# Modulation products of a two-layer diffusion trunk: fp32 in four 32-column quarters of the array, and sums of squares asked for three microseconds later

## Chip, cores and metric

The kernel runs on one core of one Trainium2 chip. The metric is the device time of one execution in microseconds (us): the median of three runs of the kernel before is 3194.48 us (3193.29 to 3196.1).

## What is computed

Two layers over 1024 latent tokens and 256 context tokens of width 1024, in fp32. Each layer modulates a normalised input with a shift, a scale and a gate that come from a condition vector: `c` for the latent tokens, `c_ctx` for the context. The parts that the change touches are the modulation and the sums of squares of the q/k normalisation:

```python
def rmsnorm(u, g):
    u32 = u.astype(jnp.float32)
    y = u32 * lax.rsqrt(jnp.mean(u32 * u32, axis=-1, keepdims=True) + EPS)
    return (y * g.astype(jnp.float32)).astype(u.dtype)

def modulation(cond, w_mod, b_mod):
    m = jax.nn.silu(cond) @ w_mod + b_mod
    shift, scale, gate = jnp.split(m, 3, axis=-1)
...
for l in range(DEPTH):
    sh_l, sc_l, gt_l = modulation(c, w_mod[l], b_mod[l])
    sh_c, sc_c, gt_c = modulation(c_ctx, w_mod[l], b_mod[l])
    h_lat = rmsnorm(x, norm_g[l]) * (1.0 + sc_l) + sh_l
    h_ctx = rmsnorm(ctx, norm_g[l]) * (1.0 + sc_c) + sh_c
    q_l, k_l, v_l, ga_l, u_l, gb_l, gm_l = split_proj(h_lat @ w_in[l])
...
    q_l = axial_rope(rmsnorm(q_l.reshape(B, n, N_Q_HEADS, HEAD_DIM), q_norm_g[l]), rows, cols) * scale
    k_l = axial_rope(rmsnorm(k_l.reshape(B, n, N_KV_HEADS, HEAD_DIM), k_norm_g[l]), rows, cols)
...
    x = x + gt_l * merge_branches(o_lat, ga_l, lru_l, gb_l, gm_l, w_a_out[l], w_b_out[l], w_out[l])
```

So a layer's modulation is a product of two condition vectors with a 1024 x 3072 weight matrix, six column blocks of 512: blocks 0 and 1 are the shift, 2 and 3 the scale, 4 and 5 the gate.

## The kernel before

Everything is laid out with features on the 128 partitions; the tokens are three chunks, L0 and L1 (512 latent tokens each) and C (256 context tokens). Large products split each fp32 operand into a high and a low fp32r part and sum three fp32r products, `gemm`, in groups of three matmuls per 128 rows of the contraction.

The stages follow each other. *Preparation* loads x and layer 0's modulation weights, normalises, modulates, and begins the q projections. Then for each layer *q/k/v*, *recurrent*, *attention* and *output* (in two halves: A for L0 and C, B for L1), with the next layer's preparation woven into the output stage.

What sets the order of the work: TensorE's order is the order in which the program emits it (`manual_schedule`). A `Timeline` counts modelled TensorE time in `tl.now`; `tl.at(delay, fn)` holds back a piece of work, and `tl.pump()` emits what is due. So a delay decides how many matmuls stand ahead of a piece on TensorE. All transfers are issued in order by one queue (SP). Buffers come from rings in turn: `mix` (four tiles) and `sm` (three); a new tile waits for the last use of the one whose place it takes.

Names and lines of the kernel before that the following speaks of:

- Preparation. `modulation` (line 318) multiplies the condition vectors `cs` (two columns of the array) with one 512-row half of a 512-column block per call, four fp32 products of 512 columns into the PSUM tile `modps`. `mod_turn` (line 332) copies the two result rows to `mrow`, and TensorE turns them by transposes into `modpt`; `mod_done` (line 307) adds the bias and makes the multipliers `ma`. Preparation does blocks 0, 2, 1, 3 from eight weight tiles `wm` of 1024 KB. `scale_rows` (line 627) makes L0's, C's and L1's sums of squares (`sqa`, `ssn`), the reciprocal roots (`rst`), their broadcast (`rb`) and scales x; `modulate` (line 662) makes the high and low operand `h` or `c`.
- Output stage. `modulation_side` (line 345) does 16 half-blocks of 256 columns: layer 0's gate (blocks 4, 5) and all six blocks of layer 1. For each, ScalarE multiplies eight weight tiles with the condition (`macc`, `wmt`, line 358), GpSimd adds them up (line 360), ScalarE and VectorE split the sum (`mhi`, `mlo`, lines 367 and 368), and TensorE sums over the partitions with four fp32r products of 256 columns. It is a generator: `weave` (line 598) takes one step of it per two groups of three matmuls in half A, and 0.36 steps per group in half B.
- q/k. `Group.evac` (line 461) copies a projection (`qg`) and squares it (`sqq`) on ScalarE; `sums` (line 476) sums the squares per head on TensorE (`ssq`) in the four 32-column quarters, 4.0 us of modelled time after the last chunk; then `qrow` goes through DRAM, `rsqrt_small` makes `rst` (line 400 is its square root on ScalarE), and `apply` (line 519) rotates and scales. `lsum` (line 1045) sums attention rows (`lps`), also in quarters.
- `recurrent_consts` (line 194) makes constants in `spt`, some 26 small VectorE instructions per layer.

Of the kernel before, what the change touches and what calls it, by code (L numbers as in the profile page):

```python
# [26 lines left out]
F32 = mybir.dt.float32  # L27
# [12 lines left out]
KT = 8  # L40
# [60 lines left out]
def trunk_kernel(ctx: ExitStack, tc: tile.TileContext, xT, cc, par, wmod, win, wgate, wo,  # L101
# [45 lines left out]
    def tr(o, a):  # L147
# [10 lines left out]
    e2 = sm("e2")  # L158
    V.memset(e2[:, 0:4], 0.0)
    V.memset(e2[:, 0:4:3], 1.0)  # L160
    cond_sel = const.tile([128, 2, 2], F32R, name="condsel")
    V.tensor_copy(cond_sel, e2[:, 0:4].rearrange("p (a b) -> p a b", a=2))
# [9 lines left out]
                    pattern=[[-1, 128]], channel_multiplier=1)  # L172

# [7 lines left out]
    cs = const.tile([128, KT, 2], F32, name="cs")  # L181
    ct = const.tile([128, KT, 2], F32, name="ct")
    S.activation(ct, cc_sb, AF.Tanh, scale=0.5)
    V.scalar_tensor_tensor(cs, ct, 1.0, cc_sb, op0=OP.add, op1=OP.mult)
    V.tensor_scalar(cs, cs, 0.5, None, op0=OP.mult)
# [8 lines left out]
    def recurrent_consts(l):  # L194
        lam = p(l, "lam", 0, 16)
        t = const.tile([128, 6, 16], F32, name="spt", tag="spt")
# [124 lines left out]
    def modulation(l, i, b, half, wm, box):  # L321

        if half == 0:
            box["ps"] = ptile("s", "modps")
        ps = box["ps"]
        for k in range(4):
            mm(ps[0:2], cs[:, 4 * half + k], wm[:, k], half == 0 and k == 0, half == 1 and k == 3)
            tl.pump()
        if half == 1:
            mod_turn(l, 4 * b, 4, ps, 1.0)  # L330

    def mod_turn(l, i, n, ps, wait):

        row = sm("mrow")
        S.activation(row[0:2, 0:n * 128], ps[0:2, 0:n * 128], AF.Copy)

        def turn():
            pt = ptile("s", "modpt")
            for j in range(n):
                tl.now += 0.109  # L340
                nc.tensor.transpose(pt[:, 2 * j:2 * j + 2], row[0:2, j * 128:(j + 1) * 128], ident[0:2, 0:2])
            mod_done(l, i, n, pt)

        tl.at(wait, turn)

    def modulation_side(l, blocks, work):

        for hb in [2 * b + i for b in blocks for i in range(2)]:
            acc = work.tile([128, 2, 256], F32, name="macc", tag="macc")
            for k in range(KT):  # L350
                if k % 4 == 0:
                    wm = mix("wm")[:, 0:1024].rearrange("p (k n) -> p k n", k=4)
                    DMA.dma_start(wm, wmod[l, k * 128:(k + 4) * 128, hb * 256:(hb + 1) * 256]
                                  .rearrange("(k p) n -> p k n", p=128))
                w = wm[:, k % 4]
                t = acc if k == 0 else sm("wmt").rearrange("p (s n) -> p s n", s=2)
                for s in range(2):
                    S.activation(t[:, s], w, AF.Copy, scale=cs[:, k, s:s + 1])  # L358
                if k:
                    G.tensor_add(acc, acc, t)  # L360
                yield

            for _ in range(4):
                yield
            hi = sm("mhi", F32R).rearrange("p (s n) -> p s n", s=2)
            lo = sm("mlo", F32R).rearrange("p (s n) -> p s n", s=2)
            S.activation(hi, acc, AF.Copy)
            V.tensor_sub(lo, acc, r32(hi))
            for _ in range(3):
                yield  # L370
            ps = ptile("av", "modps")
            for x, part in enumerate((hi, lo)):
                for s in range(2):
                    mm(ps[0:2, 0:256], cond_sel[:, s], part[:, s], x + s == 0, x + s == 2)
            mod_turn(l, 2 * hb, 2, ps, 3.0)
# [76 lines left out]
    class Group:  # L452
# [10 lines left out]
        def evac(self, i, c, ps):  # L463
            off, n = CH[c]
            if i not in self.qg:
                self.qg[i] = mix("qg")
            S.activation(self.qg[i][:, off:off + n], ps[:, :n], AF.Copy, scale=self.g)
            part = next(p_ for p_ in self.parts if c in p_)
            o = min(CH[x][0] for x in part)
            if (i, o) not in self.sq:  # L470
                self.sq[i, o] = self.work().tile([128, TOK], F32, name="sqq", tag="sqq") if self.work else mix("sqq")
            S.activation(self.sq[i, o][:, off - o:off - o + n], ps[:, :n], AF.Square)
            if c == part[-1]:
                tl.at(4.0, lambda: self.sums(i, part, o))
# [134 lines left out]
    with tc.tile_pool(name="prep", bufs=1, reuse_waits="tile") as work:  # L609
        xs, arrive = {}, {}  # L610
# [15 lines left out]
        def scale_rows(c):  # L626
# [18 lines left out]
            def bcast():  # L645
# [4 lines left out]
                for k in range(KT):  # L650
                    if c == "L1":
# [10 lines left out]
        def modulate(c, k0, nk=4):  # L662

            n = CH[c][1]
# [28 lines left out]
        for i in range(8):  # L693
            tl.now = max(tl.now, arrive[i])
            modulation(0, i, blocks[i // 2], i % 2, xs[i], box)
            if i == 4:
                tl.at(0.0, lambda: modulate("L0", 0))
            if i == 6:
                tl.at(0.0, lambda: modulate("C", 0))
# [9 lines left out]
    for l in range(DEPTH):  # L709
# [414 lines left out]
        with tc.tile_pool(name="outp", bufs=1, reuse_waits="tile") as work:  # L1124
# [128 lines left out]
            else:  # L1253
                mod_start(l + 1)
                side = modulation_side(l, (4, 5), work) if l == 0 else iter(())
                tl.fill(weave(ga, itertools.chain(side, modulation_side(l + 1, (0, 2, 1, 3), work)), 0.5))
            tl.fill(halves(1, nxt) if last else weave(halves(1, nxt), modulation_side(l + 1, (4, 5), work), 0.36))
# [79 lines left out]
```

## Time and profile before

| | |
|---|---|
| time, median of 3 runs | 3194.48 us |
| the profiled execution's own time | 3197.96 us |
| its span | 3196.2 us |
| TensorE (PE) busy | 3059.7 us, 96% |
| VectorE (DVE) busy | 2457.1 us, 77% |
| ScalarE (ACT) busy | 1749.6 us, 55% |
| GpSimd (POOL) busy | 1020.0 us, 32% |
| first projection on PE | at 51.00 us |
| output stage of layer 0, 1350 to 1610 us | PE busy 239.74 of 260.00 us |
| end of layer 1's q/k/v, 1760 to 1905 us | PE busy 134.75 of 145.00 us |

The profile is of one execution; times in it count from the start of its span. PE is busy nearly always, so what matters is where it is not, and where it runs at the lower of its two clock levels (1.2 instead of 2.4 GHz, shown as 0.50 of full speed). An engine's row names an instruction's output and inputs; an fp32 matmul appears as two records.

### The profile page before, as it was taken

What the parts mean: (1) busy time and instruction counts of PE and PEld (TensorE: products, weight loads), DVE (VectorE), ACT (ScalarE), POOL (GpSimd) and SP (SyncE); (2) the same over time, 40 slices, a digit from 0 to 9 for tenths busy, and PEclk for the clock granted to TensorE, in tenths of its full rate; (3) what the DMA queues carried; (4) which work ended last, traced back from release to release, by engine and by line L of the source; (5) the groups of instructions that cost most, each with busy time, mean ns of one, the idle gap of its engine ahead of it and who ended that gap; (6) DMA issues with size and microseconds to landing.
All of it is one profiled execution on the core that took longest, in us unless ns stands there. A gap on an engine that the chain in (4) does not pass through costs nothing. (4 is left out here: it accounts for less than half of the span.)

```text
span 3196.2 us, 42921 instructions
## 1 busy us (share of the span) xinstructions
PE 3059.7 (96%) x14880; PEld 2430.8 (76%) x14880; DVE 2457.1 (77%) x3675; ACT 1749.6 (55%) x3060; POOL 1020.0 (32%) x777
## 2 busy tenths in 40 slices
PE   7999999999999999999899999899999999999999
PEld 3788788777777777787778778777777777777887
DVE  7665887589898988556685785997799999996544
ACT  4323667466666666545555324676477766673222
POOL 0211444234434333234432121433244444441000
PEclk9999999999999999999999999999999999999999
DMA  5443111311222122264555452111412121115554
GB/s 196 144 152 121 50 50 62 115 59 59 73 64 78 60 64 64 87 195 153 172 191 168 147 166 87 60 47 53 121 56 75 58 75 58 52 59 170 181 177 138
DMA packets 233049, 331.95 MB, mean 104 GB/s; under 512 B 53296, under 2 KB 99184, under 8 KB 232576
## 3 DMA queue, kind: packets, MB, share of 16 engines
q1 hardware_dynamic: 232832, 329.21, 32.0%
q8 instruction: 117, 1.92, 0.2%
q14 instruction: 100, 0.82, 0.1%
HBM read 252.54 MB, written 76.58 MB: 103 GB/s over the span
## 5 line engine op out<-in xcount | busy, mean ns | idle before, releaser
L145 PE MATMUL gps<-h,whi 128*128 128x512 f32 x3328 | 1041.4, 394 | 21.1 <-DVE g L876 15.3
L145 PEld LDWEIGHTS gps<-h,whi 128*128 128x128 f32 x3328 | 612.1, 190 | 148.4 <-issue 10.7
L1004 DVE TENSOR_TENSOR pl<-pf,ph 128x512 fp32r<-128x512 f32 x656 | 630.2, 961 | 83.1 <-ACT ph L1003 79.5
L145 PE MATMUL gps<-h,wlo 128*128 128x512 f32 x1664 | 654.5, 393 | 1.3 <-DVE wlo L227 1.3
L1002 ACT ACTIVATE pf<-s2ps 128x512 f32<-128x512 f32 x656 | 392.8, 599 | 348.1 <-issue 157.0
L1018 POOL TENSOR_TENSOR acc<-pf 128x512 f32<-128x512 f32 x256 | 352.0, 1375 | 713.1 <-ACT pf L1002 711.5
L980 DVE TENSOR_REDUCE mp<-s1ps 128x1 f32<-128x512 f32 (+1 forms) x800 | 454.1, 583 | 63.7 <-PE s1ps L145 60.8
L1003 ACT ACTIVATE ph<-s2ps 128x512 fp32r<-128x512 f32 x656 | 390.0, 595 | 0.0
L227 DVE TENSOR_TENSOR wlo<-wraw,whi 128x512 fp32r<-128x512 f32 x392 | 335.3, 878 | 61.4 <-ACT whi L226 32.7
L226 ACT ACTIVATE whi<-wraw 128x512 fp32r<-128x512 f32 x324 | 193.6, 627 | 333.8 <-PE gps L145 258.1
L145 PEld LDWEIGHTS gps<-h,wlo 128*128 128x128 f32 x1664 | 314.3, 189 | 69.9 <-DVE wlo L227 2.0
L145 PE MATMUL s1ps<-k,qa 128*128 128x512 f32 (+1 forms) x800 | 284.9, 363 | 12.3 <-DMA qa<-q0L 10.3
L145 PE MATMUL avps<-ph,vv 128*128 128x512 f32 x656 | 266.9, 407 | 0.0
L145 PE MATMUL avps<-pl,vv 128*128 128x512 f32 x656 | 260.2, 397 | 5.0 <-DVE pl L1004 4.9
L145 PE MATMUL s2ps<-qa,k 128*128 128x512 f32 x656 | 261.1, 398 | 1.8 <-DVE mp L980 1.6
L145 PE MATMUL s2ps<-qb,k 65*128 65x512 f32 x656 | 260.3, 397 | 0.0
L145 PE MATMUL gps<-e,whi 128*128 128x512 f32 x768 | 243.9, 399 | 0.2 <-DVE e L227 0.2
L360 POOL TENSOR_TENSOR macc<-macc,wmt 128x512 f32<-128x512 f32 x112 | 156.2, 1395 | 255.2 <-ACT wmt L358 221.9
L145 PE MATMUL qps<-h,whi 128*128 128x512 f32 x640 | 203.0, 398 | 1.5 <-DVE h L674 0.9
L1020 POOL TENSOR_TENSOR acc<-acc,pf 128x512 f32<-128x512 f32 x128 | 181.5, 1418 | 71.4 <-ACT pf L1002 69.2
L145 PE MATMUL gps<-c,whi 128*128 128x256 f32 x1024 | 197.2, 288 | 3.1 <-DVE c L222 2.1
L145 PEld LDWEIGHTS s1ps<-k,qa 128*128 128x128 f32 x800 | 151.6, 190 | 51.8 <-issue 6.4
(216 smaller groups left out, 5026.6 us busy)
## 6 DMA issues: line engine op xcount, KB each, us to landing
wraw<-in_win_dram SPq DMA_DIRECT2D x200, 256.0 KB
wraw<-in_wo_dram SPq DMA_DIRECT2D x192, 256.0 KB
wm<-in_wmod_dram SPq DMA_DIRECT2D x32, 512.0 KB
wm<-in_wmod_dram SPq DMA_DIRECT2D x8, 1024.0 KB
rb<-rq SPq DMA_DIRECT2D x64, 128.0 KB
k<-k SPq DMA_DIRECT2D x24, 320.0 KB
v<-vst SPq DMA_DIRECT2D x20, 256.0 KB
vv<-v SPq DMA_DIRECT2D x8, 640.0 KB
```

The source lines that it names most:

```text
L145: nc.tensor.matmul(o, a, b, start=start, stop=stop)
L226: S.activation(dst_hi, src, AF.Copy)
L227: (V if lo_eng == "v" else G).tensor_sub(dst_lo, src, r32(dst_hi))
L360: G.tensor_add(acc, acc, t)
L980: tl.at(0.3, lambda: V.reduce_max(self.mp[:, j, b:b + 1], ps[:, :n], axis=AX.X))
L1002: S.activation(pf, ps, AF.Exp)
L1003: S.activation(ph, ps, AF.Exp)
L1004: tl.at(1.4, lambda: V.tensor_sub(pl, pf, r32(ph)))
L1018: G.tensor_add(self.acc_tile(x), first, pf)
L1020: G.tensor_add(self.accs[x], self.accs[x], pf)
```

## The change

- Both modulations become fp32 products with `csp`, the condition padded with zeros to 32 columns. Four products, one per 128 rows, go to the four 32-column quarters of the array and leave four partial results on PSUM partitions 0, 32, 64 and 96. `mrow` is now 128 rows, and the turn is an fp32 product of `mrow` with `sel4`, which adds the four parts.
- In the output stage ScalarE's scaling, GpSimd's additions and the high/low split go; each half-block is two weight tiles loaded a few steps earlier, eight products of 256 columns, and the turn. A half-block takes 14 steps of the generator instead of 15.
- `sums` is asked for 7.0 instead of 4.0 us after the last chunk.
- In preparation `modulate("L0", 0)` comes after call 5 instead of 4 and `modulate("C", 0)` after the last call.
- `cs`, `ct` and `spt` come from the `sm` ring, so the small VectorE instructions of `recurrent_consts` run in each layer's q/k stage instead of at the start of the kernel.

```diff
-    e2 = sm("e2")
-    V.memset(e2[:, 0:4], 0.0)
-    V.memset(e2[:, 0:4:3], 1.0)
-    cond_sel = const.tile([128, 2, 2], F32R, name="condsel")
-    V.tensor_copy(cond_sel, e2[:, 0:4].rearrange("p (a b) -> p a b", a=2))
...
+    sel4 = const.tile([128, 2], F32, name="sel4")
+    V.reduce_sum(sel4, ident.rearrange("p (g s) -> p s g", s=32)[:, 0:2], axis=AX.X)
...
-    cs = const.tile([128, KT, 2], F32, name="cs")
-    ct = const.tile([128, KT, 2], F32, name="ct")
+    cs, ct = (sm(n_)[:, 0:16].rearrange("p (k s) -> p k s", k=KT) for n_ in ("cs", "ct"))
     S.activation(ct, cc_sb, AF.Tanh, scale=0.5)
     V.scalar_tensor_tensor(cs, ct, 1.0, cc_sb, op0=OP.add, op1=OP.mult)
-    V.tensor_scalar(cs, cs, 0.5, None, op0=OP.mult)
+    csp = const.tile([128, KT, 32], F32, name="csp")
+    V.memset(csp, 0.0)
+    V.tensor_scalar(csp[:, :, 0:2], cs, 0.5, None, op0=OP.mult)
...
-        t = const.tile([128, 6, 16], F32, name="spt", tag="spt")
+        t = sm("spt")[:, 0:96].rearrange("p (a b) -> p a b", a=6)
...
-    def modulation(l, i, b, half, wm, box):
-
+    def mod_half(ps, half, wm, n):
+
+        for k in range(4):
+            mm(ps[32 * k:32 * k + 32, :n], csp[:, 4 * half + k], wm[:, k], half == 0, half == 1, 0.215 * n / 512)
+
+    def modulation(l, b, half, wm, box):
         if half == 0:
             box["ps"] = ptile("s", "modps")
-        ps = box["ps"]
-        for k in range(4):
-            mm(ps[0:2], cs[:, 4 * half + k], wm[:, k], half == 0 and k == 0, half == 1 and k == 3)
-            tl.pump()
+        mod_half(box["ps"], half, wm, 512)
+        tl.pump()
         if half == 1:
-            mod_turn(l, 4 * b, 4, ps, 1.0)
+            mod_turn(l, 4 * b, 4, box["ps"], 1.0)
     def mod_turn(l, i, n, ps, wait):
         row = sm("mrow")
-        S.activation(row[0:2, 0:n * 128], ps[0:2, 0:n * 128], AF.Copy)
+        S.activation(row[:, 0:n * 128], ps[:, 0:n * 128], AF.Copy)
         def turn():
             pt = ptile("s", "modpt")
             for j in range(n):
-                tl.now += 0.109
-                nc.tensor.transpose(pt[:, 2 * j:2 * j + 2], row[0:2, j * 128:(j + 1) * 128], ident[0:2, 0:2])
+                mm(pt[:, 2 * j:2 * j + 2], row[:, j * 128:(j + 1) * 128], sel4, True, True, 0.2)
             mod_done(l, i, n, pt)
         tl.at(wait, turn)
-    def modulation_side(l, blocks, work):
+    def modulation_side(l, blocks):
         for hb in [2 * b + i for b in blocks for i in range(2)]:
-            acc = work.tile([128, 2, 256], F32, name="macc", tag="macc")
-            for k in range(KT):
-                if k % 4 == 0:
-                    wm = mix("wm")[:, 0:1024].rearrange("p (k n) -> p k n", k=4)
-                    DMA.dma_start(wm, wmod[l, k * 128:(k + 4) * 128, hb * 256:(hb + 1) * 256]
-                                  .rearrange("(k p) n -> p k n", p=128))
-                w = wm[:, k % 4]
-                t = acc if k == 0 else sm("wmt").rearrange("p (s n) -> p s n", s=2)
-                for s in range(2):
-                    S.activation(t[:, s], w, AF.Copy, scale=cs[:, k, s:s + 1])
-                if k:
-                    G.tensor_add(acc, acc, t)
-                yield
-
+            wms = []
+            for half in range(2):
+                wm = mix("wm")[:, 0:1024].rearrange("p (k n) -> p k n", k=4)
+                DMA.dma_start(wm, wmod[l, half * 512:half * 512 + 512, hb * 256:(hb + 1) * 256]
+                              .rearrange("(k p) n -> p k n", p=128))
+                wms.append(wm)
+                for _ in range(3):
+                    yield
             for _ in range(4):
                 yield
-            hi = sm("mhi", F32R).rearrange("p (s n) -> p s n", s=2)
-            lo = sm("mlo", F32R).rearrange("p (s n) -> p s n", s=2)
-            S.activation(hi, acc, AF.Copy)
-            V.tensor_sub(lo, acc, r32(hi))
-            for _ in range(3):
+            ps = ptile("av", "modps")
+            for half in range(2):
+                mod_half(ps, half, wms[half], 256)
+            mod_turn(l, 2 * hb, 2, ps, 3.0)
+            for _ in range(4):
                 yield
-            ps = ptile("av", "modps")
-            for x, part in enumerate((hi, lo)):
-                for s in range(2):
-                    mm(ps[0:2, 0:256], cond_sel[:, s], part[:, s], x + s == 0, x + s == 2)
-            mod_turn(l, 2 * hb, 2, ps, 3.0)
...
-                tl.at(4.0, lambda: self.sums(i, part, o))
+                tl.at(7.0, lambda: self.sums(i, part, o))
...
-            modulation(0, i, blocks[i // 2], i % 2, xs[i], box)
-            if i == 4:
+            modulation(0, blocks[i // 2], i % 2, xs[i], box)
+            if i == 5:
                 tl.at(0.0, lambda: modulate("L0", 0))
-            if i == 6:
-                tl.at(0.0, lambda: modulate("C", 0))
+        tl.at(1.0, lambda: modulate("C", 0))
         tl.at(1.2, lambda: modulate("L0", 4))
         tl.at(4.0, lambda: modulate("C", 4))
...
-                side = modulation_side(l, (4, 5), work) if l == 0 else iter(())
-                tl.fill(weave(ga, itertools.chain(side, modulation_side(l + 1, (0, 2, 1, 3), work)), 0.5))
-            tl.fill(halves(1, nxt) if last else weave(halves(1, nxt), modulation_side(l + 1, (4, 5), work), 0.36))
+                side = modulation_side(l, (4, 5)) if l == 0 else iter(())
+                tl.fill(weave(ga, itertools.chain(side, modulation_side(l + 1, (0, 2, 1, 3))), 0.5))
+            tl.fill(halves(1, nxt) if last else weave(halves(1, nxt), modulation_side(l + 1, (4, 5)), 0.36))
```

The rows are in each engine's own order. TensorE in preparation (`modps` modulation products, `modpt` turns, `ssn` sums of squares, `rb` their broadcast, `qps` the first projection). Before:

```order
L145 MATMUL ssn<-ones,sqa 128x1 x4
L145 MATMUL modps<-wm,cs 2x512 x2
L145 MATMUL rb<-ident,rst 128x128 x4
L145 MATMUL modps<-wm,cs 2x512 x2
L341 MATMUL modpt<-ident,mrow 128x2 x4
L145 MATMUL modps<-wm,cs 2x512 x7
L341 MATMUL modpt<-ident,mrow 128x2 x4
L145 MATMUL ssn<-ones,sqa 128x1 x2
L145 MATMUL modps<-wm,cs 2x512 x2
L145 MATMUL rb<-ident,rst 128x128 x2
L145 MATMUL modps<-wm,cs 2x512 x5
L145 MATMUL qps<-h_530,whi 128x512
```

and now:

```order
L145 MATMUL ssn<-ones,sqa 128x1 x4
L145 MATMUL modpt<-sel_91,mrow 128x2 x4
L145 MATMUL rb<-ident,rst 128x128 x4
L145 MATMUL modps<-wm,csp 32x512 x8
L145 MATMUL modpt<-sel_91,mrow 128x2 x4
L145 MATMUL ssn<-ones,sqa 128x1 x2
L145 MATMUL modps<-wm,csp 32x512 x4
L145 MATMUL rb<-ident,rst 128x128 x2
L145 MATMUL qps<-h_539,whi 128x512
L145 MATMUL qps<-h_540,whi 128x512
L145 MATMUL qps<-h_539,wlo 128x512
L145 MATMUL modpt<-sel_91,mrow 128x2 x4
```

L0's `ssn` now has five of the eight weight tiles' products ahead of it (20 products, where 14 were), the turn of block 2 stands ahead of `rb`, and the last turn follows the first group of the projection.

TensorE in the output stage, around the first half-block (`gps` are the output products of C; the half-block's turn follows later). Before:

```order
L145 MATMUL gps<-c_13880,whi 128x256
L145 MATMUL gps<-c_13879,wlo 128x256
L145 MATMUL modps<-mhi,condsel 2x256 x2
L145 MATMUL modps<-mlo,condsel 2x256 x2
L145 MATMUL gps<-c_13879,whi 128x256
```

and now, one such place some 33 matmuls earlier:

```order
L145 MATMUL gps<-c_13879,whi 128x256
L145 MATMUL gps<-c_13878,wlo 128x256
L145 MATMUL modps<-wm,csp 32x256 x8
L145 MATMUL gps<-c_13878,whi 128x256
L145 MATMUL gps<-c_13879,whi 128x256
```

The products no longer read `mhi` and `mlo` but the loaded weight tile `wm`, and there are eight of them at a time.

ScalarE at the end of layer 1's q/k/v (`qg` and `sqq` copy and square the last k projection, `rst` is the square root of a norm that went through DRAM, `vst` copies v). Before:

```order
L467 ACTIVATE qg<-qps,par 128x512
L472 ACTIVATE sqq<-qps 128x512
L467 ACTIVATE qg<-qps,par 128x256
L472 ACTIVATE sqq<-qps 128x256
L400 ACTIVATE rst<-rst 128x20
L467 ACTIVATE qg<-qps,par 128x512
L472 ACTIVATE sqq<-qps 128x512
L764 ACTIVATE vst<-vps 128x4x64
```

and now:

```order
L388 ACTIVATE rst<-rst 128x16
L455 ACTIVATE qg<-qps,par 128x512
L460 ACTIVATE sqq<-qps 128x512
L471 ACTIVATE qrow<-ssq 128x320
L455 ACTIVATE qg<-qps,par 128x256
L460 ACTIVATE sqq<-qps 128x256
L455 ACTIVATE qg<-qps,par 128x512
L460 ACTIVATE sqq<-qps 128x512
L388 ACTIVATE rst<-rst 128x20
L753 ACTIVATE vst<-vps 128x4x64 x2
```

The last `qg` and `sqq` of 512 columns stood behind the second `rst` and now stand ahead of it.

## Rows read from the trace of the kernel before

**Rows 1.** Whom PE waited for, whole span (us in total, times, longest us).

```profile
PE ssq L145 <- ACT sqq L472: 16.8, 6, 7.8
PE modps L145 <- ACT mhi L367: 9.1, 6, 4.8
PE modps L145 <- DVE mlo L368: 5.6, 6, 2.6
```

**Rows 2.** Timeline of PE, output stage: first and last of those twelve waits.

```profile
1458.50 0.59 PE L145 MATMUL modps<-mhi,condsel 128*2 128x256 f32 x2 [4.80 <-ACT mhi L367]
1608.64 0.40 PE L145 MATMUL modps<-mlo,condsel 128*2 128x256 f32 x2 [0.41 <-DVE mlo L368]
```

**Rows 3.** Stretches after a PE wait: busy times, granted clock (PEclk), DMA.

```profile
1458.50:1463.30 4.80, 4.57 (x21) 3.98 (x22) 2.22 (x5) 3.40 (x8) 1.20 (x1) 0.50 0.18 61
1552.00:1559.00 7.00, 5.99 (x26) 5.71 (x27) 3.49 (x7) 2.41 (x6) 0.00 (x0) 0.51 0.47 164
1897.40:1903.40 6.00, 6.00 (x26) 4.97 (x27) 6.00 (x15) 1.03 (x3) 2.07 (x3) 0.50 0.28 104
```

**Rows 4.** Timeline of ScalarE and PE, end of layer 1's q/k/v (idle before).

```profile
1884.02 0.22 ACT L400 ACTIVATE rst<-rst 128x16 f32<-128x16 f32 x1 [12.71 <-issue]
...
1896.06 0.22 ACT L400 ACTIVATE rst<-rst 128x20 f32<-128x20 f32 x1 [9.80 <-issue]
...
1897.39 1.28 PE L145 MATMUL ssq<-sqq,sel 128*32 128x320 f32 x4 [7.80 <-ACT sqq L472]
```

**Rows 5.** Timeline, preparation and the start of the projections, in order of time.

```profile
22.29 1.28 ACT L400 ACT_TABLE_LOAD   x1
...
28.04 4.87 DVE L654 TENSOR_TENSOR xsL<-xsL,rb 128x512 f32<-128x512 f32 x8 [1.69 <-PE rb L145]
...
51.00 0.74 PE L145 MATMUL qps<-h,whi 128*128 128x512 f32 x2
...
80.31 0.53 PE L145 MATMUL ssq<-sqq,sel 128*32 128x192 f32 x8 [2.97 <-ACT sqq L472]
...
86.56 0.62 PE L145 MATMUL qps<-h,whi 128*128 128x512 f32 x2
```

**Rows 6.** VectorE in preparation (busy time, count, PE's clock, DMA).

```profile
28.00:83.00 55.00, 46.42 (x107) 0.89 0.31 111
```

**Rows 7.** Groups of PE, preparation (busy, mean ns, idle before and releaser).

```profile
L145 PE MATMUL modps<-wm,cs 128*2 128x512 f32 x64 | 33.5, 672 | 7.2 <-DVE spt L207 7.0 <-DMA wm<-in_wmod_dram 0.3
```

**Rows 8.** Timeline of PE: prices of fp32 products and what starts behind them.

```profile
24.05 1.05 PE L145 MATMUL ssn<-ones,sqa 128*128 128x1 f32 x8 [1.22 <-DVE sqa L395]
...
715.07 1.06 PE L145 MATMUL lps<-acc,ones 128*32 128x512 f32 x8
716.06 0.50 PE L145 MATMUL avps<-ph,vv 128*128 128x512 f32 x1
...
1402.65 0.39 PE L145 MATMUL modps<-mhi,condsel 128*2 128x256 f32 x2
...
1403.12 0.40 PE L145 MATMUL gps<-c,whi 128*128 128x256 f32 x2
...
1823.87 0.63 PE L145 MATMUL ssq<-sqq,sel 128*32 128x256 f32 x4 [0.58 <-ACT sqq L472]
1824.42 0.73 PE L145 MATMUL qps<-h,whi 128*128 128x512 f32 x2
```

**Rows 9.** Groups of PE, output stage: the turns of the 16 half-blocks.

```profile
L341 PE MATMUL modpt<-ident,mrow 2*128 2x2 f32 x32 | 4.5, 208 | 0.2 <-ACT mrow L335 0.2
```

**Rows 10.** Timeline, output stage: a weight tile's issue on SP and first use.

```profile
1350.29 0.38 SPq L353 DMA_DIRECT2D wm<-in_wmod_dram  x1
...
1354.25 0.91 ACT L358 ACTIVATE macc<-wm,cs 128x256 f32<-128x256 f32 x2 [2.53 <-DMA wm<-in_wmod_dram]
```

**Rows 11.** SP's own waits, 1350 to 1760 us (us in total, times, longest).

```profile
SPq L1171 <- ACT wmt L358: 30.4, 9, 6.0
```

**Rows 12.** The `spt` instructions alone, first 15 us (VectorE and ScalarE busy).

```profile
0.00:15.00 15.00, 8.78 (x52) 0.43 (x2) 1.00 0.88 309
```

More of the change, by code (lines that the diff above doesn't have):

```diff
@@ L609, in trunk_kernel @@
     with tc.tile_pool(name="prep", bufs=1, reuse_waits="tile") as work:
-        xs, arrive = {}, {}
+        xs, arrive, scaled = {}, {}, set()
         mod_start(0)
@@ L650, in bcast @@
                 for k in range(KT):
+                    scaled.add(c)
                     if c == "L1":
@@ L662, in modulate @@
         def modulate(c, k0, nk=4):
+            assert c in scaled
             n = CH[c][1]
```

## Prediction

> **What bounds the kernel now.** I read the waits of TensorE first, since it is busy 96% of the span: a gain is either a wait that goes, matmul time that shrinks, or time at the lower clock that is won back. Over the whole span three of its waits bear on this change [rows 1]. In the output stage the half-blocks' products wait for `mhi` 9.1 us in all and for `mlo` 5.6 us, twelve waits; the timeline shows the first of them at 1458.50 with 4.80 us, the last at 1608.64 [rows 2]. The reader should see who is late: the sum of scaled weights passes from ScalarE to GpSimd eight times and back, and TensorE, in order, stands with all output products queued behind it. In the q/k stages `ssq` waits for `sqq` 16.8 us in six waits, the longest 7.8 us.
>
> The stretches behind long waits come next [rows 3]: the granted clock is 0.50 of full speed, its 1.2 GHz level, after TensorE stood idle up to 1458.50, and again from 1552 and from 1897. So such a wait costs more than itself.
>
> Third, the 7.8 us wait [rows 4]. ScalarE is held at `rst` until 1884.02 (12.71 us) and again until 1896.06 (9.80 us), and the last square that `ssq` needs stands behind that second `rst`. TensorE starts again at 1897.39.
>
> Last, preparation [rows 5, 6, 7]. The 64 records of modulation products keep TensorE busy 33.5 us, and the projections begin at 51.00; but VectorE works 46.42 of the 55 us from 28 to 83, from the scaling of L0 to the last low part of L1, and the first tile's L1 product, which needs all of that, ends only at 86.56. I take VectorE to be the limit there.
>
> **The change, part by part.** All is summed against the profiled execution's 3197.96 us, which lies 3.48 us above the median of the three runs, and then moved down by that.
>
> *Output stage, what goes.* What the twelve waits were for goes: 9.1 + 5.6 = 14.7 us. The lost clock behind them: busy 4.57 us at 0.50 and 5.99 us at 0.51 [rows 3], so 4.57 x 0.50 + 5.99 x 0.49 = 5.2 us; a third such stretch is left out. ScalarE's scalings, GpSimd's additions and VectorE's `mlo` lie beside TensorE's other work and count for nothing more, though their relief may shorten other waits of this stage; I leave that to the range.
>
> *Output stage, what comes.* Eight fp32 products of 256 columns in quarters, per visit. Rows of that form exist [rows 8]: a set of four of 256 columns takes 1824.42 - 1823.87 = 0.55 us (`ssq`), a set of four of 512 takes 716.06 - 715.07 = 0.99 us (`lps`). So a column costs 1.72 ns per set and a set has 0.11 us beside. Two sets: 1.10 us. The old four products took 1403.12 - 1402.65 = 0.47 us: +0.63 us. The turn was 4.5 us for 16 visits [rows 9], 0.28 each; two fp32 products with a full stationary tile, at 1.05 / 4 = 0.26 each by `ssn` [rows 8], make 0.53: +0.25. Together +0.88 us x 16 = +14.1 us, all on TensorE's path. The stage's sum is -14.7 - 5.2 + 14.1 = **-5.8 us**; call it -6.
>
> Here a rule is to be weighed. The rows cannot tell whether the 0.11 us is paid for each set of four or once for each entry into quarters, since every set in the trace stands alone among full-array products. The Trainium skill, TensorEngine Tiling (Array Packing), Key Properties, says that changing the tiling mode drains the engine, while changing the tile does not. It speaks against the change, which enters and leaves that mode 16 more times in this stage; but it also says that two adjacent sets pay once. By it a visit would be 0.99 us and the sum -7.6 us instead of -5.8; no run here shows two sets in a row. I keep 1.10.
>
> The weight tiles must be there when the products come. A tile issued at 1350.29 was first used at 1354.25 after a wait for it [rows 10], so 4.0 us. The second tile is asked for 7 of 14 steps ahead; twelve visits took 1402.65 to 1608.64, about 18 us each, so roughly 8.7 us ahead at 14/15 of that pace. I cost this wait at nothing, with 4.7 us of cover; what happens without it is a rival.
>
> *Sums asked for later.* Of the 16.8 us, 2.97 are in preparation [rows 5] and counted there; 13.8 are left in five waits, and 6.00 us at 0.50 behind the longest lose 3.0 us. Three microseconds more of matmuls ahead of each `ssq` cover the four short waits (6.0 us together). For the long one: at the least 3 us go, the rest and the clock stay. At the most all 7.8 + 3.0 go, since in the changed order the last square stands ahead of the second `rst`, and has only to follow the first, released at 1884.02; the seven ScalarE instructions from there to the last square should be over before TensorE arrives, at 1897.39 - 7.80 + 3 = 1892.6. So 9.0 to 16.8 us; I take **-15**, near the upper end because of that order. The transfers behind `ssq` (`qrow` out and back on SP) move with it and the rotation on VectorE ends later; behind them stand the next tiles' weights, which are asked for two tiles ahead, and the recurrent stage, which needs no q or k. If that cover failed, it would come out as waits of the next tiles, up to the 3 us per shift.
>
> *Constants moved.* VectorE does 8.78 us of small `spt` instructions in the first 15 us [rows 12]; 4.4 us per layer now fall into q/k stages, and ScalarE must reload its function table twice per layer, 1.28 us each [rows 5]. Covered by VectorE's idle time there (the stage's VectorE is not what TensorE waits for) and by the 3 us that `ssq` gained. Zero; 7 us per layer at the worst, which the upper bound takes in part.
>
> *Preparation.* Eight calls fall from 33.5 us of TensorE to a set of four each, 0.99 us, or twice that at 1.2 GHz. But VectorE has the same instructions, 55 us from the scaling of L0 on. Its start cannot come sooner: `ssn` now stands behind one weight tile more and a turn stands ahead of `rb`, 0.99 + 1.05 us, doubled at the low level 4.1. The gain: some of VectorE's 8.6 us of idle time in that stretch ended on TensorE's products, and the 2.97 us wait of `ssq` may go; 3 us at the most. So -3 to +4; I take **+1**.
>
> Sum: -6 - 15 + 1 = -20. 3197.96 - 20 = 3178.0 profiled, **3174.5 us** as a median. About 0.2% (6.4 us) is what a measurement of this kernel can tell from no change.
>
> **Rivals.**
>
> *The late square stays late (0.17).* The first `rst` moves with its sums, later by 3 us or more, and holds ScalarE as long as before. For it: ScalarE was held twice in a row [rows 4], which is a slow chain through DRAM and not one accident. Against it: the order. The lower end, -9, applies: 3180.5 us.
>
> *Preparation was bound by TensorE (0.08).* For it: projections begin only at 51.00. Then the products' fall, and the 4 half-speed ones among them, brings the whole chain forward, -8 instead of +1: 3165.5 us. Against it: VectorE's 46 of 55 us.
>
> *Slower: the weight tiles come late (0.07).* They take places in the four-tile ring, each now held until TensorE has used it, where ScalarE gave it back. SP is in order, so a transfer that waits for such a place holds all that follow. SP's waits for places held by `wmt` were nine, 3.4 us in the mean and 6.0 at the longest [rows 11]. One longest and one mean in each visit, 9.4 us, exceed the 4.7 us of cover by 4.7: twelve visits, 56 us. 3174.5 + 56 = 3230.5 us. It decides from 4.7 + 20 / 12 = 6.4 us of holding per visit. Against it: each place is given back at a visit, some 17 us before the next needs its products, and `mrow`'s and GpSimd's delays on the same ring vanish.
>
> *The quarters do not overlap (0.03).* Each 256-column product would cost alone what a set without its 0.11 costs, 0.44: 3.52 per visit, +38.7 us over the 1.10 in 16 visits; 3213 us. `lps` and `ssq` speak against it.
>
> **How the numbers follow.** Forecast 0.65: 3174.5 us. Its own bounds are -35 (preparation -3, output -15 by shortened other waits, sums -17) to -5 (+4, 0, -9), 3159.5 to 3189.5. That range also takes in the first two rivals and leaves out the slow ones and the tails: 3159 to 3190. Faster by over 0.2% means under 3188.1: nearly all of the forecast, three quarters of the first rival, the second: 0.84. Slower: the last two, 0.10. Within: 0.06.
>
> **What would show it.** In the profile after, no wait of `modps` for ScalarE or VectorE in the output stage, and a visit of eight products at 1.0 to 1.1 us; a larger visit would break the second term. The PE's clock at 1.00 from 1450 to 1600. `ssq` waiting under 5 us in all, none above 3; if one of 4 us or more stands at the end of layer 1's q/k, the first rival holds. The second tile's L1 product starting at 84 to 91 us (86.56 now). Waits of `modps` for `wm` transfers would mean the slow rival. The prediction is wrong if the output stage does not get shorter, or if preparation moves by more than 4 us.

## The result and the profile after

The changed kernel takes **3176.02 us** (median of 4 runs, 3175.5 to 3178.79); the kernel before, beside it, 3195.29 us (3193.29 to 3199.36). The ratio is 0.9940, 95% interval 0.9923 to 0.9957: faster by more than the 0.2% that can be told from no change, 1.5 us from the predicted 3174.5 and inside the range. The profiled execution took 3175.98 us, span 3174.1. The runs below show that the sum was right and that none of its four terms was.

The engines' busy times, from the page. PE is busy 8 us less than the 3059.7 of before; ScalarE lost 111 us of work and GpSimd 156.

```profile
PE 3051.5 (96%) x15120; PEld 2436.6 (77%) x15120; DVE 2404.5 (76%) x3658; ACT 1638.3 (52%) x2792; POOL 864.5 (27%) x665
```

Whom PE waited for, whole span (us in total, times, longest), the lines that answer to [rows 1]:

```profile
PE gps L145 <- DVE g L865: 18.1, 11, 3.3
...
PE modps L145 <- DMA wm<-in_wmod_dram: 13.9, 5, 7.3
...
PE ssn L145 <- DVE sqa L383: 11.2, 2, 9.0
...
PE vps L145 <- DVE vst L754: 2.4, 1, 2.4
PE ssq L145 <- ACT qrow L471: 2.3, 1, 2.3
...
PE ssq L145 <- ACT sqq L460: 1.4, 1, 1.4
```

The waits for `mhi` and `mlo` are gone with the tiles. All five waits of `modps` for `wm` are in preparation: none is in the output stage, so the weight tiles are never late there. `ssq` waits 3.7 us in all where it waited 16.8. New are the 9.0 us of `ssn` and the 2.4 us of `vps`.

Two stretches of windows, first the output stage from its first product to the first projection of layer 1 (busy times of PE, PEld, DVE, ACT, POOL, then granted clock):

```profile
1362.77:1738.56 375.79, 369.15 (x2073) 303.88 (x2072) 198.47 (x384) 97.64 (x181) 0.00 (x0) 0.99 0.56 181
```

In the kernel before the same stretch, from 1363.89 to 1755.21, is 391.32 us long with PE busy 365.99 at 0.97. So 18.7 us of idle time went and 3.2 us of busy time came: 15.5 us shorter in these two executions.

A visit on PE's timeline, answering to [rows 8]:

```profile
1394.97 0.28 PE L145 MATMUL gps<-c,wlo 128*128 128x256 f32 x1
1395.18 1.07 PE L145 MATMUL modps<-wm,csp 128*32 128x256 f32 x16
1396.18 0.50 PE L145 MATMUL gps<-c,whi 128*128 128x256 f32 x2
```

The eight products take 1396.18 - 1395.18 = 1.00 us. The turns of the stage:

```profile
L145 PE MATMUL modpt<-sel,mrow 128*128 128x2 f32 x64 | 8.1, 232 | 0.6 <-ACT mrow L335 0.6
```

That is 0.51 us for each of 16.

Preparation on the timeline, answering to [rows 5]:

```profile
25.35 1.87 PE L145 MATMUL ssn<-ones,sqa 128*128 128x1 f32 x8
27.08 1.85 PE L145 MATMUL modpt<-sel,mrow 128*128 128x2 f32 x8
...
30.15 2.04 PE L145 MATMUL rb<-ident,rst 128*128 128x128 f32 x8 [1.23 <-DVE rst L392]
...
32.23 4.87 DVE L643 TENSOR_TENSOR xsL<-xsL,rb 128x512 f32<-128x512 f32 x8 [2.23 <-PE rb L145]
...
46.01 0.98 PE L145 MATMUL ssn<-ones,sqa 128*128 128x1 f32 x4 [9.04 <-DVE sqa L383]
...
49.66 1.20 PE L145 MATMUL qps<-h,whi 128*128 128x512 f32 x2
...
89.30 0.50 PE L145 MATMUL qps<-h,whi 128*128 128x512 f32 x1 [1.26 <-DVE h L664]
89.64 0.40 PE L145 MATMUL qps<-h,wlo 128*128 128x512 f32 x1
89.87 0.62 PE L145 MATMUL qps<-h,whi 128*128 128x512 f32 x2
```

VectorE begins to scale L0 at 32.23 where it was 28.04. `ssn` of the context stands 9.04 us behind VectorE, in the middle of preparation. The first projection starts 1.3 us sooner than before, but the first tile's L1 product now waits for VectorE at 89.30, in the last of its eight groups of three, and the second tile's begins at 89.87. In the kernel before that product began at 87.92:

```profile
80.77 1.06 PE L145 MATMUL qps<-h,whi 128*128 128x512 f32 x2
...
86.56 0.62 PE L145 MATMUL qps<-h,whi 128*128 128x512 f32 x2
...
87.24 0.62 PE L145 MATMUL qps<-h,whi 128*128 128x512 f32 x2
...
87.92 0.62 PE L145 MATMUL qps<-h,whi 128*128 128x512 f32 x2
```

The row at 86.56, which the prediction took for it, is the seventh of the first tile's eight groups: 80.77 is the first, 87.24 the eighth. So this product starts 1.95 us later than before.

And the clock there, the 25 us from 35 on (kernel after, windows; the same stretch of the kernel before had PE busy 19.42 us at 0.86):

```profile
35.00:60.00 25.00, 14.65 (x55) 10.05 (x51) 21.17 (x54) 16.30 (x32) 0.00 (x0) 0.66 0.39 137
```

### The profile page after: what moved, and what is told of

The parts are those of the page before. It is cut to its first block, busy times and chain, and to the rows that moved or that the text cites. A ratio compares the mean times of both kernels' runs of the same rounds, so it can differ in the third digit from the quotient of the medians.

```text
span 3174.1 us, 42865 instructions
## 1 busy us (share of the span) xinstructions
PE 3051.5 (96%) x15120; PEld 2436.6 (77%) x15120; DVE 2404.5 (76%) x3658; ACT 1638.3 (52%) x2792; POOL 864.5 (27%) x665
## 3 DMA queue, kind: packets, MB, share of 16 engines
q8 instruction: 119, 1.95, 0.3%
## 5 line engine op out<-in xcount | busy, mean ns | idle before, releaser
L225 DVE TENSOR_TENSOR wlo<-wraw,whi 128x512 fp32r<-128x512 f32 x392 | 310.8, 816 | 41.7 <-ACT whi L224 21.2
L518 POOL TENSOR_TENSOR t<-qg,rc 128x512 f32<-128x512 f32 x40 | 61.2, 1529 | 705.5 <-DMA rc<-in_ropec_dram 515.4
```

The source lines that it names most:

```text
L225: (V if lo_eng == "v" else G).tensor_sub(dst_lo, src, r32(dst_hi))
L518: G.tensor_mul(t1, a, rc[:, o:o + n])
```

## The experiments

Times are ratios to the kernel before, run on the same chip; us are the ratio's distance times 3195.3. A ratio's interval is about 0.0014 to either side, so two ratios differ with some 0.002 (6 us) of doubt. Single traces move too: in two executions of the unaltered changed kernel the last matmul ends at 3170.30 and 3178.00. So the medians give the sizes, and the traces say where, each for one execution. The time at which a stage begins is that of its first product: `vps` for the values, `gtps` for the recurrent stage's gates.

**Sums of squares early again** (no_later_sums): in the changed kernel,

```diff
-                tl.at(7.0, lambda: self.sums(i, part, o))
+                tl.at(4.0, lambda: self.sums(i, part, o))
```

> The changed kernel with its sums of squares asked for at 4.0 again. My step of the forecast (the shift is worth 15 us, both layers): 12 to 17 us longer than the changed kernel, about 3190. Rival, from the landmarks of the two traces (the stage q/k of layer 0 gained 8.3 us, but the recurrent stage of layer 0 began only 0.5 us sooner): the gain of layer 0 is swallowed, only that of layer 1 counts, 8 to 11 us, about 3185, and TensorE's first gtps stays within 1.5 us of 299.7. Both expect ssq to wait for sqq 12 us or more again, with one wait of 6 us or more at the end of layer 1's q/k.

0.9959 (0.9945 to 0.9974). Against the mean of the changed kernel's two measurements (0.9940 and, below, 0.9934) this is 0.0022, 7 us longer: the shift is worth half of my 15. `ssq` waits 10.8 us again, the longest 5.3, a little under what both theories expected; that longest wait (1851.05) stands 33 us ahead of the last one of layer 1, which is 1.08. The first `gtps` is at 302.41 where the changed kernel has 299.70, so not within the 1.5 us of the rival: here some of layer 0's gain is kept.

**Only the later sums** (only_later_sums): the opposite edit of the same line in the kernel before.

> The kernel before with its sums of squares asked for at 7.0, nothing else changed. If the parts add: 9 us (the rival above) to 15 us (my step) shorter than before. If the shift gives its gain only where the other parts freed the engines: under 4 us shorter. The first gtps at 300 +- 1.5 if the recurrent stage's start is set by something else than TensorE; at 295 if by TensorE.

0.9983 (0.9972 to 0.9995): 5.4 us shorter, between the two expectations, more than the 4 of the one and less than the 9 of the other. The first `gtps` is at 300.16, as before to the hundredth, though the stage of values had begun 7.0 us sooner (210.51 for 217.51). In this execution the gain in q/k is lost on the way to `gtps`, in two waits (timeline of this kernel; `gr` are the recurrent stage's gate weights, from which GpSimd makes `gh` and VectorE `gl`):

```profile
229.61 0.22 ACT L400 ACTIVATE rst<-rst 128x20 f32<-128x20 f32 x1 [12.11 <-issue]
...
230.65 0.39 PE L145 MATMUL vps<-wvh,h 128*128 128x256 f32 x1 [1.93 <-DVE vst L765]
...
263.05 0.36 SPq L565 DMA_DIRECT2D k<-qhl  x1
263.50 6.11 SPq L781 DMA_DIRECT2D gr<-in_wgate_dram  x2
...
268.15 1.09 DVE L227 TENSOR_TENSOR gl<-gr,gh 128x512 fp32r<-128x512 f32 x1 [5.13 <-POOL gh L224]
...
281.42 0.41 DVE L876 SCALAR_TENSOR_TENSOR g<-gbt,gps 128x256 f32<-128x256 f32 x1
...
281.89 0.74 PE L145 MATMUL gps<-h,whi 128*128 128x512 f32 x2 [2.17 <-DVE g L876]
```

and in the kernel before:

```profile
229.66 0.22 ACT L400 ACTIVATE rst<-rst 128x20 f32<-128x20 f32 x1 [10.77 <-issue]
...
262.07 0.36 SPq L565 DMA_DIRECT2D k<-qhl  x1
...
263.08 10.57 SPq L781 DMA_DIRECT2D gr<-in_wgate_dram  x3
...
283.04 0.41 DVE L876 SCALAR_TENSOR_TENSOR g<-gbt,gps 128x256 f32<-128x256 f32 x1
...
283.51 0.73 PE L145 MATMUL gps<-h,whi 128*128 128x512 f32 x2 [0.53 <-DVE g L876]
```

TensorE comes sooner, but what it meets there doesn't. The norm's chain through DRAM ends where it did (`rst` at 229.61 for 229.66), and ScalarE's and VectorE's copies of v stand behind it. The gate weights are asked for right behind the last rotated k in the one queue, at 263.50 for 263.08. VectorE isn't late by its own work: it stood idle 5.13 us for `gh`, and it reaches the row of `g` shown 1.6 us sooner than before, where TensorE comes 3.3 us sooner. The two waits are 1.93 and 1.64 us (2.17 for 0.53), 3.6 of the 7.0; the rest goes at the lower clock behind them, 0.89 from 225 to 240, 0.93 from 270 to 285 and 0.96 from 285 to 300, where the kernel before has 1.00. The wait for `g` is 3.26 us in the changed kernel, and 1.14 in the one with its sums early again.

**Preparation as it was** (old_prep): the changed kernel with the old products, turn (kept beside the new one as `mod_turn_old`) and places of the modulating steps in preparation; `cs` has a tile of its own again and takes no place in the `sm` ring.

```diff
-        mod_half(box["ps"], half, wm, 512)
-        tl.pump()
+        for k in range(4):
+            mm(ps[0:2], cs[:, 4 * half + k], wm[:, k], half == 0 and k == 0, half == 1 and k == 3)
+            tl.pump()
...
-            mod_turn(l, 4 * b, 4, box["ps"], 1.0)
+            mod_turn_old(l, 4 * b, 4, ps, 1.0)
...
-            if i == 5:
+            if i == 4:
...
-        tl.at(1.0, lambda: modulate("C", 0))
+            if i == 6:
+                tl.at(0.0, lambda: modulate("C", 0))
```

> The changed kernel with preparation's modulation as it was (two-column products, turn by transposes, modulating steps where they were), the rest as changed. Theory: the new preparation costs time, since VectorE's chain is the limit and starts 4 us later (32.2 where it was 28.0): here the projections' second tile starts its L1 product near 86.5 instead of 90, and the whole is 2 to 4 us shorter than the changed kernel if later stages carry it, 0 +- 1.5 if the recurrent stage of layer 0 swallows it as it swallowed the gain in q/k. Rival (TensorE was the limit in preparation): 2 to 8 us longer.

0.9915 (0.9898 to 0.9933): faster than the changed kernel, by more than the theory said. The second tile's L1 product begins at 84.53, 5.3 us before the changed kernel's, and the stage of values at 207.36 for 212.71; the first `gtps` is 2.8 us sooner, at 296.87. The granted clock is the other difference:

```profile
35.00:60.00 25.00, 18.94 (x61) 7.61 (x60) 21.42 (x54) 17.26 (x33) 0.00 (x0) 0.93 0.39 134
```

PE is busy longer here than in the changed kernel (18.94 us for 14.65) and runs at 0.93 for 0.66 (0.86 in this kernel's second run, below). The old, slower products kept the engine at work through the stretch in which it otherwise stands waiting for `sqa`.

**The output stage as it was** (old_side): the changed kernel with the old scaling on ScalarE, additions on GpSimd, `mhi` and `mlo`.

```diff
-            for half in range(2):
-                mod_half(ps, half, wms[half], 256)
-            mod_turn(l, 2 * hb, 2, ps, 3.0)
...
+            for x, part in enumerate((hi, lo)):
+                for s in range(2):
+                    mm(ps[0:2, 0:256], cond_sel[:, s], part[:, s], x + s == 0, x + s == 2)
+            mod_turn_old(l, 2 * hb, 2, ps, 3.0)
```

> The changed kernel with the output stage's modulation as it was (ScalarE scales, GpSimd adds, hi and lo products), the rest as changed. Theory: the stage is worth what the landmarks show, so 14 to 18 us longer than the changed kernel (about 3191), with waits of modps for mhi and mlo of 12 us or more and the granted clock down to 0.5 in two or three places again. Rival, my own step: 6 us longer (about 3182), the rest of the 15.5 us between the landmarks coming from something else.

0.9976 (0.9964 to 0.9987): 0.0039 or 12.5 us longer than the changed kernel, and not 6. The waits come back (PE, whole span):

```profile
PE modps L145 <- ACT mhi L387: 8.3, 4, 3.9
...
PE modps L145 <- DVE mlo L388: 3.5, 6, 1.6
```

11.8 us of them, a little under the 12 expected, and the clock falls again: 0.97 from 1440 to 1490, 0.93 from 1540 to 1590, where the changed kernel has 1.00.

**The changed kernel again** (after_again), unaltered:

> The changed kernel unaltered, as the measure for the others on this chip. All theories: 0.994 of the kernel before, within its interval (0.9923 to 0.9957).

0.9934 (0.9920 to 0.9948).

**L0's root first** (root_first): in the new preparation, `ssn` of L0 ahead of the fourth weight tile's products, its `rb` ahead of the turn.

```diff
-                tl.at(5.0 if c != "C" else 3.5, sums2)
+                tl.at(4.0 if c == "L0" else (5.0 if c == "L1" else 3.5), sums2)
...
-                tl.at(2.5, bcast)
+                tl.at(1.0 if c == "L0" else 2.5, bcast)
```

> The changed kernel with L0's sum of squares (ssn) put ahead of the fourth tile's products and its rb ahead of the turn that now precedes it. Theory (the new preparation costs because VectorE's scaling of L0 starts at 32.2 where it was 28.0): it starts at 28.5 to 29.5, the wait of ssn of C (9.0 us) is shorter by about as much, the stage of values starts 2 to 4 us sooner than the 212.7 of the changed kernel, and the whole is 2 to 6 us shorter. Rival (the loss is TensorE's low clock from 40 to 60, for want of work, and not VectorE's start): the granted clock of 40 to 60 stays near 0.5 to 0.67 and the whole changes by under 2 us.

0.9928 (0.9913 to 0.9942): 2 to 3 us, which is not to be told from nothing. VectorE starts scaling at 28.10, the wait of the context's `ssn` is 6.40 instead of 9.04, values begin at 210.22; but the clock from 35 to 60 stays at 0.67. Each theory has a part of the trace for it, and the time does not decide between them.

**Work in the gap** (filled): six sets of products on a tile that is there, ahead of the context's `ssn`; nothing reads their bank.

```diff
+                if c == "C":
+                    idle = ptile("s", "idle")
+                    for _ in range(3):
+                        mod_half(idle, 0, xs[7], 512)
+                        tl.now -= 0.86
+                        mod_half(idle, 1, xs[7], 512)
+                        tl.now -= 0.86
```

> The changed kernel with 24 more products (six sets of the modulation's form on a tile that is there anyway, into a bank that nobody reads) ahead of the ssn of C, where TensorE waits 9.0 us. Theory (VectorE's late start is the loss): nothing is gained, 0 to 4 us longer. Rival (low clock): the granted clock of 45 to 60 rises from about 0.55 to 0.9 or more, ssn, rb and the first projections run at full speed, and the whole is 2 to 6 us shorter although it does more.

0.9935 (0.9922 to 0.9947): no change. It tells little, since 4.91 us of the wait were left and the clock fell to 0.69 (40 to 50) all the same. It had to be tried with the shorter gap.

**The small constants alone** (only_spt): in the kernel before,

```diff
-        t = const.tile([128, 6, 16], F32, name="spt", tag="spt")
+        t = sm("spt")[:, 0:96].rearrange("p (a b) -> p a b", a=6)
```

> The kernel before with the small spt work moved into the q/k stages as in the changed kernel, nothing else. My step: 0 +- 2 us. Rival, from the sum of the parts measured so far (shift about 6, output stage about 12, preparation about 8 the other way: 10 of the 19 us): the missing 9 us are this move's, 5 to 10 us shorter than before, by VectorE being free in the first 15 us. If it is 0, the parts don't add and the rest is in how they act together.

0.9982 (0.9972 to 0.9993): 5.8 us shorter (2 to 9 by the interval), by an edit that I had costed at nothing. It is not won at the start: there PE's first products waited 7.0 us for `spt` on VectorE [rows 7], and now they wait as long for the first weight tile. What its trace shows beside that are the waits of `ssq`:

```profile
PE ssq L145 <- ACT sqq L472: 12.3, 5, 5.0
...
PE modps L145 <- DMA wm<-in_wmod_dram: 7.1, 1, 7.1
```

16.8 us became 12.3 with the sums where they were, and the last wait of layer 1, 7.80 us [rows 4], is 0.20. A 5.04 us wait stands 33 us ahead of it, at 1863.02, so that TensorE arrives later at the last one, which begins 1.3 us sooner than before (1896.10 for 1897.39). This trace can't size the gain: its execution took 3199.80 us, the longest of the eleven and 1.8 us longer than the profiled one of the kernel before.

**Preparation as it was, once more** (old_prep_again):

> The same kernel as old_prep once more, beside others on one chip. Theory (the new preparation costs 6 us): 0.9915 of the kernel before within its interval (0.9898 to 0.9933), below the 0.9934 of the unaltered changed kernel. Rival (the first result was chance): 0.993 to 0.995.

0.9915 (0.9901 to 0.9928), the same again. With both pairs of runs: 0.9937 for the changed kernel, 0.9915 with the old preparation, 7 us with some 5 us of doubt. The new preparation costs time, and this kernel is the best of all that ran: 3172.0 us beside 3195.9 (in the first run 3168.8 beside 3198.3).

**Both edits to the new preparation** (root_filled), so root_first and filled together:

> Both earlier edits to the new preparation at once: ssn and rb of L0 first, and 24 more products into an unread bank where TensorE then still waits 6.4 us. Theory (the 6 us are half VectorE's late start and half the low clock behind an idle TensorE): the granted clock of 35 to 60 is above 0.9, the stage of values starts 4 to 6 us sooner than the 212.7 to 214.0 of the changed kernel, and the whole is 3 to 6 us shorter. Rival (the clock there does not matter, since VectorE sets the pace): no more than the 2 us of the first edit alone, or none.

The clock of 35 to 60 rises from root_first's 0.67 to 0.86, not to the 0.9 expected, and the stage of values begins at 206.22, 6.5 and 7.8 us sooner than in the changed kernel's two traces, as early as with the old preparation (207.36 and 209.42). The windows of this kernel:

```profile
35.00:60.00 25.00, 19.36 (x117) 12.63 (x108) 22.16 (x57) 16.87 (x32) 0.00 (x0) 0.86 0.39 136
20.00:100.00 80.00, 68.71 (x384) 47.82 (x385) 61.50 (x144) 41.73 (x80) 3.33 (x3) 0.96 0.42 144
```

From 20 to 100 the clock is 0.96; the changed kernel has 0.87 and 0.85 there, root_first 0.83. So in this execution 24 useless products, which fill a wait, make the projections end sooner. The median is 0.9931 (0.9918 to 0.9943), though, 2 us better than the changed kernel with 6 us of doubt: what the trace shows at 206 us is not confirmed by the whole time. (The profiled execution, 3172.57 us, was 2.7 us faster than this kernel's median.)

**Output stage and constants alone** (side_and_spt): old_prep with its sums at 4.0.

> The changed kernel with the old preparation and the sums of squares at 4.0: so the kernel before with the new output stage and the moved spt work alone. If the parts add, with the output stage at 13 us and the spt move at 6: 19 us shorter than before, 0.994. If the parts hide one another (the shift's gain is the same time as one of theirs): 0.992. By my own steps (output stage 6, spt 0): 0.998.

0.9940 (0.9928 to 0.9953), 19.2 us. Less the 5.8 of `spt` this gives 13.4 for the output stage; and to old_prep, which has the later sums beside, there are 0.0025 or 8 us. As far as 6 us of doubt lets one see, the parts add.

**The two sets of a visit apart** (apart):

```diff
-            for half in range(2):
-                mod_half(ps, half, wms[half], 256)
+            mod_half(ps, 0, wms[0], 256)
+            yield
+            mod_half(ps, 1, wms[1], 256)
```

> The changed kernel with three or more products of the output stage between the two sets of four of each visit. If what a set has beside its columns (0.11 us) is paid once for each entry into quarters, as one visit of 1.00 us suggests: the two sets take 0.55 us each, 1.10 a visit instead of 1.00. If it is paid for each set, as I had summed it: no change of what a set takes, 0.50 each. Whole: within 3 us.

PE's timeline of this kernel:

```profile
1396.78 0.64 PE L145 MATMUL modps<-wm,csp 128*32 128x256 f32 x8
1397.35 0.51 PE L145 MATMUL gps<-c,whi 128*128 128x256 f32 x2
...
1398.60 0.64 PE L145 MATMUL modps<-wm,csp 128*32 128x256 f32 x8
1399.17 0.51 PE L145 MATMUL gps<-e,whi 128*128 128x512 f32 x1
```

Each of the 32 sets now takes 0.57 us, a visit 1.14, where each of the changed kernel's 16 visits takes 1.00: what a set has beside its columns, 0.14 us, is paid per entry. (Its one time, 3183.95 us, says nothing of 2 us.)

The move of the constants was measured from one side alone, in the kernel before; no run undoes it in the changed kernel.

## Why the prediction was right, and why its steps were not

| term | forecast | measured | from |
|---|---|---|---|
| output stage | -6 | -12.5 to -13.4 | old_side; side_and_spt less only_spt |
| sums later | -15 | -5.4 to -8 | only_later_sums; no_later_sums; old_prep less side_and_spt |
| constants moved | 0 | -5.8 | only_spt |
| preparation | +1 | +7 | old_prep, twice |
| sum | -20 | -18.3 with -12.5, -7, -5.8, +7 | the kernel itself: -19.2 and -21.1 |

The time came out within 1.5 us by luck: two errors of 6 us for the worse (too little for the output stage, nothing for the constants) stood against two of 6 and 8 us for the better. Each measured term has a doubt of some 4 to 6 us of its own.

*Output stage.* The mechanism was right: no wait of the half-blocks' products for ScalarE or VectorE, and a clock of 1.00 from 1450 to 1600, where it had been 0.94 with stretches at 0.50. The size failed in what I left out. I counted twelve waits, 14.7 us; 18.7 us of idle time went, since the relief of ScalarE and VectorE shortened others (`rb` behind `rst` from 4.38 us at 1648.04 to 0.98 at 1630.60). "Left to the range" meant zero in the sum. The work that came was +0.53 a visit and +0.23 a turn, 12.2 us for 14.1; PE's busy time grew by 3.2 only, so by this difference the clock gave back about 9 us, where I had counted two of its stretches, 5.2. Here the rule that I weighed is decided: the Trainium skill, TensorEngine Tiling (Array Packing), Key Properties, says that changing the tiling mode drains the engine while changing the tile does not, and the traces agree in the price, with 1.00 us for two sets together and 0.57 for each alone. Its 0.99 was the better price than my 1.10.

*Sums later.* "Near the upper end because of that order" was wrong in two ways. The long wait of layer 1, with its clock 10.8 us of the 15, shrinks by the constants' move as well, which alone takes it to 0.20 us with a wait of 5.04 us before it; the shift cannot be credited with all of it. And the step "the recurrent stage, which needs no q or k" failed: it needs the transfer queue. Its gate weights are asked for behind the last rotated k, and the copies of v stand behind the norm's `rst`; in only_later_sums neither moved with TensorE. By the shift the stage of values of layer 0 begins 4.2 to 7.7 us sooner (no_later_sums against the changed kernel, only_later_sums against the kernel before, side_and_spt against old_prep), but the first `gtps` only 2.7, 0.0 and 2.5 us; in layer 1 `vps` waits 2.39 us anew. Of the points to be shown, those on `ssq` hold (3.7 us in all, none over 2.3); they were not what decides. The rival of the late square fell: it stands ahead of the second `rst`, as the order said.

*Constants.* "Zero" rested on cover for their cost and never asked what their leaving might give. How their 5.8 us come about stays open: the waits of `ssq` are 4.5 us shorter in a trace that isn't faster. The move also gives `spt` a place in the `sm` ring, so that the tiles behind it fall to other places; no run separates that from the relief of VectorE.

*Preparation.* The chain was read rightly, but for the row at 86.56: VectorE's start moved by 4.2 us where I had 4.1 as the worst. But the worst was the case, and I netted it against a gain that did not come. What the sum lacked altogether is that cheaper products leave PE idle there, and that the clock is then lower, 0.66 for 0.86 from 35 to 60. The runs root_first and root_filled show each half of it by its trace; that their medians do not gain 5 us stays unexplained, so the 7 us are measured and this cause of them is argued. What else old_prep puts back, the turn and the place of `cs` in the ring, was not tried alone. By the prediction's own last sign it is wrong if preparation moves by more than 4 us: by 7, with some 5 of doubt, it did, if one goes by the time; the second tile's product moved by 1.95. The rival that TensorE bounds preparation is refuted, with the opposite sign.

In the output stage no product waited for a weight tile, and the quarters do overlap (eight products in 1.00 us), so both slower rivals fell.

## What to carry to other kernels

Where a change touches several stages, price each from its own rows in both directions, also the part that "only moves": here each of four terms was off by some 6 to 8 us and the sum by 1.5. Work taken from an engine in a stretch where it is not the limit may cost time: here the products became cheaper, the engine idled, its clock was lower, and the kernel was 7 us longer than with the old ones; look at what the engine will wait for next before calling it a gain. And follow a gain to the next stage's waits before adding it up: where the engine comes sooner and the transfers it will need do not, the gain is partly borrowed.

## What was not expected of the hardware

With 24 products into a bank that nobody reads, in a gap of 6.4 us, the granted clock of 35 to 60 was 0.86 instead of 0.67 (root_first) and the stage of values began 4.0 us sooner (206.22 for 210.22), in one trace of each; the medians do not tell the two apart. Moving 52 small instructions out of the first 15 us of VectorE made the kernel 5.8 us faster, and the first products started no sooner (the first projection at 51.40 for 51.00). And two executions of one program (the changed kernel's) differ by 1.7 us at 300, by 0.2 at 599 and by 7.7 at the end, so that a single trace cannot size an edit of this kind.
